# A planned two-layer trunk: decay products in halves, statistics from a copy, a norm with another last tile, and PSUM reads ordered in the plan

## The chip, the cores and the metric

The kernel runs on one core of a Trainium2 chip. The metric is device microseconds of one execution, lower is better. TensorE is called PE below, VectorE DVE, ScalarE ACT, SyncE SP; PSUM is the buffer into which PE writes and from which DVE and ACT read.

## The reference

Two layers of a trunk run on 128 context tokens and 512 latent tokens of width 1024, float32. A layer is a modulated norm, one wide input projection, three mixers side by side (attention A, gated DeltaNet B, chunked gMLP C), a gated merge and an output projection. What the change touches:

```python
def _rms(x, g):                       # the norm ahead of a layer
    y = xf * lax.rsqrt(jnp.mean(xf * xf, axis=-1, keepdims=True) + EPS)

def _gdn_chunk(q, k, v, g, beta, s0): # B, per head: decays from cumulated gates, then a scan over chunks
    gc = jnp.cumsum(blk(g), axis=-1)
    ...
    def step(S, xs): ...
    S, o = lax.scan(step, s0, (qc, kc, u, w, gc, decay))

def _chunk_mlp(u, v, p):              # C: mean and variance over 512 channels of each token
    mu = jnp.mean(vf, axis=-1, keepdims=True)
    var = jnp.mean(jnp.square(vf - mu), axis=-1, keepdims=True)
    vn = ((vf - mu) * lax.rsqrt(var + EPS) * p['cm_ln_g'] + p['cm_ln_b'])
```

## The kernel before

All 640 tokens are the columns of every tile, in two halves of 320 (HF) where a PSUM bank of 512 columns asks for it, or in five groups of 128. The dense products of the projections (tiles `dn`) are three matmuls of 128x320 each (`hh` with `hi`, `hl` with `hi`, `hh` with `lo`), since a float32 factor is split into a rounded part and a rest. They make up most of PE's work, and they are laid between the small products of the mixers, whose inputs come from chains over DVE and ACT.

The program isn't issued as it is written. Every call is recorded (class Recorder). `add` notes for each operation which earlier ones it must follow: those that touch the same part of a tile where one of the two writes. `cost` gives it a duration, and `plan` runs a list of ready operations per engine against these durations, priorities from the place in the program, and the number of buffers of each tile name. `issue` then emits them engine by engine in the planned order, all from line 371, so that a profile tells operations apart by their tiles alone. On the chip an engine works through its order without change, and semaphores hold an instruction until its inputs and its buffer are there. Tiles of PSUM come in three kinds with two buffers each: `dn` (dense), `mm` (small products) and `p` (two banks; `p2()` in the code). A PSUM tile counts as one whole in `add` (box, line 93).

Places that the change touches:

- `gdn_head` (line 908), once per head, four per layer. For its decays PE multiplies triangular masks scaled by the gates (G, four tiles) with a constant (`c_strict`) into one `p` tile, in pieces of 512 and 128 columns; ACT takes the exponential of all 640. Then q and k of the head are transposed into `p` tiles (p_687 and p_688 in the rows below), whose squares ACT sums (`junk`, five each) before the next products of the head, p_698, can take the buffer that p_687 leaves. The scan of the head before runs at the same time: products Q and qkv, Q and G, V and G into `mm` tiles (mm_624 to mm_638), each waiting for DVE or ACT.
- The gMLP statistics (lines 1224 to 1236): for five groups of tokens PE transposes four tiles `ya` into a `dn` tile, DVE takes mean and variance from it (`bn_stats`, then `bn_aggr`), and ACT copies it to a tile D in SBUF.
- `norm_add` (line 711) squares a tile on ACT and adds it on DVE to a sum, for all tiles but the first and the last; the last square stays by itself, and `norm_end` (line 721) adds up both over the channels on PE. At the end of a layer the new tiles come in pairs from `two_blocks`, and the last pair is 6 and 7.
- Attention is untouched in the text. There a tile `p` is read by DVE (`G<-p,l_q_col,c_ropeT`) and by ACT (two squares, `G<-p 64x640` and `32x640`).

Of the kernel before, what the change touches and what calls it, by code (L numbers as in the profile page):

```python
# [10 lines left out]
AF = mybir.ActivationFunctionType  # L11
# [7 lines left out]
HF = 320  # L19
KM = 8  # L20
# [39 lines left out]
class Recorder:  # L60
# [57 lines left out]
    def add(self, eng, meth, args, kw):  # L118
        op = Op()
        op.n, op.eng, op.meth, op.args, op.kw = len(self.ops), eng, meth, args, kw  # L120
        op.prio = op.n - self.off
        op.preds, op.succs, op.tiles = set(), [], []
        outs, ins = [], []
        for i, x in enumerate(args):
            if isinstance(x, bass.AP):
                (outs if i == 0 else ins).append(x)
        for k, x in kw.items():
            if isinstance(x, bass.AP):
                (outs if k == "accum_out" else ins).append(x)
        for w, aps in ((False, ins), (True, outs)):  # L130
            for ap in aps:
                nm = ap.tensor.name
                if nm not in self.tag:
                    continue
                p0, p1, m = self.box(ap)
                lst = self.acc.setdefault(nm, [])
                keep = []
                for a_ in lst:
                    q, qw, q0, q1, qm = a_
                    hit = (w or qw) and q0 < p1 and p0 < q1 and (m & qm)  # L140
                    if hit and q is not op:
                        op.preds.add(q.n)
                    if not (w and p0 <= q0 and q1 <= p1 and (qm & ~m) == 0 and q is not op and q.eng != "SP"):
                        keep.append(a_)
                keep.append((op, w, p0, p1, m))
                self.acc[nm] = keep
                u = self.users.setdefault(nm, [])
                if not u or u[-1] is not op:
                    u.append(op)
                if nm not in op.tiles:  # L150
                    op.tiles.append(nm)
        self.cost(op, outs, ins)
        self.ops.append(op)
# [269 lines left out]
def trunk_kernel(ctx: ExitStack, tc: tile.TileContext, a, o, depth=DEPTH, dump=None):  # L423
    nc = tc.nc
    rec = Recorder(tc)
    V, S, G, PE, SY = (rec.engine(e) for e in ("V", "S", "G", "PE", "SP"))
# [16 lines left out]
    def p1():  # L443
        return T([P, 512], "mm", pool=ps, bufs=2)
# [4 lines left out]
    def X(tag, shape, dt=F32):  # L449
        return T(shape, tag, dt, bufs=NB[tag])  # L450
# [11 lines left out]
    def R(shape):  # L462
        return X("R", shape)
# [20 lines left out]
    strict = T([P, 2, P], "c_strict", F32R, pool=const)  # L484
# [223 lines left out]
    STREAMS = ((0, NL, 0), (NL, NT, 1))  # L708


    def norm_add(k):

        if k == 0:
            nsum[0] = X("C", [P, NT])
        sq = nsum[0] if k == 0 else X("C", [P, NT])
        S.activation(sq, xt[k], AF.Square)
        if 0 < k < KM - 1:
            V.tensor_tensor(nsum[0], nsum[0], sq, ALU.add)
        return sq

# [67 lines left out]
    def layer(l, md, hh, hl, fill, side):  # L788
# [46 lines left out]
        pt = p1()  # L835
# [72 lines left out]
        def gdn_head(h, qT, kT, vT):  # L908
# [3 lines left out]
            pd = p2()  # L912
            for d in range(2):
                c_ = 4 * d + h
                gx = [X("G", [P, 5, P], F32R), X("G", [P, 5, P], F32R)]
                for t in range(5):
                    S.activation(gx[0][:, t, :], masks[:, (LE, GE)[d], :], AF.Copy, scale=gh.bitcast(F32)[:, t, c_ : c_ + 1])
                V.tensor_tensor(gx[1], masks[:, (LE, GE)[d], :].unsqueeze(1).broadcast_to([P, 5, P]), gl[:, :, c_ : c_ + 1].broadcast_to([P, 5, P]), ALU.mult)
                for n in range(2):
                    gf = gx[n].rearrange("p a b -> p (a b)")  # L920
                    for c0, c1 in ((0, 512), (512, 640)):
                        PE.matmul(pd[:, c0:c1], strict[:, d, :], gf[:, c0:c1], start=(d == 0 and n == 0), stop=(d == 1 and n == 1))
            Bc = X("G", [P, 5, P])
            S.activation(Bc.rearrange("p a b -> p (a b)"), pd[:, 0:640], AF.Exp)


            junk = T([P, P], "junk", bufs=1)
# [89 lines left out]
            for step in range(4):  # L1017
                for d in range(2):
                    t = step if d == 0 else 3 - step
# [38 lines left out]
            for t0, t1 in ((0, 4), (4, 5)):  # L1058
                n = (t1 - t0) * P
# [163 lines left out]
        with rec.hp():  # L1223
            vnt = []
            mv = T([P, 5, 2], "mv", bufs=1)
            for t in range(5):
                pt = pdense()
                for q in range(4):
                    PE.transpose(pt[:, q * P : (q + 1) * P], gv[q][:, t * P : (t + 1) * P], ident)
                st6 = T([P, 6], "st6", bufs=2)  # L1230
                V.bn_stats(st6, pt)
                V.bn_aggr(mv[:, t, :], st6)
                vx = X("D", [P, 512])
                S.copy(vx, pt)
                vnt.append(vx)
            lv = R([P, 5])
            V.tensor_scalar(lv, mv[:, :, 1], 4.0 * EPS, None, ALU.add)
            lrs = rsqrt(lv, R([P, 5]), R([P, 5]))
            for t in range(5):
                V.tensor_scalar(vnt[t], vnt[t], mv[:, t, 0:1], lrs[:, t : t + 1], ALU.subtract, ALU.mult)  # L1240
# [21 lines left out]
        for q in range(4):  # L1262
            zc = silu_block(B_ZC + q, "D")
            V.tensor_tensor(cu[q], cu[q], zc, ALU.mult)
            for t0, t1 in ((0, 4), (4, 5)):
                n, cs = t1 - t0, slice(t0 * P, t1 * P)
# [150 lines left out]
        pt = p1()  # L1417
# [219 lines left out]
        for m in range(KM):  # L1637
            xo = X("qkv", [P, NT])
            SY.dma_start(xo, xsrc[m])
            xn = T([P, NT], f"ya{m}", bufs=1)  # L1640
            if m % 2 == 0:
                outs = []
            outs.append((xn, xo))

            def evac(i, acc, c0, c1):
                xn, xo = outs[i]
                cuts = ((0, c1, 0),) if c0 == 0 else ((c0, NL, 0), (NL, c1, 1))
                mi = m - m % 2 + i
                for b0, b1, s in cuts:
                    V.scalar_tensor_tensor(xn[:, b0:b1], acc[:, b0 - c0 : b1 - c0], md.gate[:, mi, s : s + 1], xo[:, b0:b1], ALU.mult, ALU.add)  # L1650

            if m < 2:
                dense(wsplit(wo(m, 0)) + wsplit(wo(m, 1)), yh, yl, lambda acc, c0, c1: evac(m, acc, c0, c1))
                done = [m]
                if m == 1:
                    B = sums()
            elif m % 2 == 0:
                continue
            else:
                two_blocks([wo(m - 1 + i, half) for i in range(2) for half in range(2)], B, evac)  # L1660
                done = [m - 1, m]
            for n in done:
                xn = outs[n % 2][0]
                if last:
                    SY.dma_start(o["y"][:, n, :], xn)
                else:
                    xt[n] = xn
                    xsrc[n] = spill(xn)
                    sq = norm_add(n)
        return None if last else sq  # L1670


# [16 lines left out]
    for k in range(KM):  # L1689
        sq = norm_add(k)  # L1690
# [10 lines left out]
    for l in range(depth):  # L1701
# [3 lines left out]
        sq = layer(l, mods[l], [h[0] for h in hs], [h[1] for h in hs], fill, side)  # L1705
# [104 lines left out]
```

## Time and profile before

| | |
|---|---|
| time, median of 3 runs | 1702.54 us (1701.52 to 1705.32) |
| the profiled execution | 1704.07 us |
| its span, first to last instruction | 1702.3 us |
| mean granted clock of TensorE | 0.987 |
| PE busy | 1646.9 us (97%) |
| DVE busy | 1287.8 us (76%) |
| ACT busy | 884.9 us (52%) |

The profiled execution took 1.8 us more than its span, and 1.5 us more than the median. Busy time is a sum over the whole span. How the engines stand in one stretch is told by the windows, and what an engine waited for by the idle time ahead of an instruction, with the one that released it. A granted clock of 1 is 2.4 GHz, of 0.5 1.2 GHz.

### The profile page before, as it was taken

The numbers are of one execution on the slowest core, as the hardware profiler recorded it, in microseconds if no ns is written. First come the engines' busy times: TensorE is split into PE (matmuls) and PEld (weight loads), VectorE is DVE, ScalarE is ACT, GpSimd is POOL, SyncE is SP. The second block draws the span as 40 slices with busy tenths as digits, with TensorE's granted clock in tenths as the row PEclk, the third lists the DMA queues.
The fourth block names the chain that finished last, engine by engine and source line by source line (L and its number), as shares of the span: only waits on it lengthen the run. The fifth ranks groups of instructions, "written<-read, shape, count | busy, mean of one in ns | idle before, by whom it ended". The sixth has DMA issues, their size and how long they took to land.

```text
span 1702.3 us, 34983 instructions
## 1 busy us (share of the span) xinstructions
PE 1646.9 (97%) x13286; PEld 1538.8 (90%) x13286; DVE 1287.8 (76%) x3638; ACT 884.9 (52%) x2201; POOL 16.6 (1%) x100
## 2 busy tenths in 40 slices
PE   6999999999999999999999999999999999999998
PEld 5998988999888889999989989889988888899998
DVE  4898888565655777887987988885656557779898
ACT  3566665554544554444445676645545445545453
POOL 0000000000000000000000000000000000000000
PEclk9999999999999999999989999999999999999999
DMA  9311211221111213564542212112221122123252
GB/s 295 99 54 51 62 57 44 70 63 59 47 58 49 84 59 107 157 201 153 189 154 59 61 42 62 57 57 64 69 59 40 53 63 74 52 83 101 85 168 80
DMA packets 94617, 146.39 MB, mean 86 GB/s; under 512 B 14064, under 2 KB 38000, under 8 KB 94448
## 3 DMA queue, kind: packets, MB, share of 16 engines
q1 hardware_dynamic: 94448, 144.15, 27.5%
q8 instruction: 105, 1.72, 0.4%
q14 instruction: 64, 0.52, 0.1%
HBM read 132.28 MB, written 11.83 MB: 85 GB/s over the span
## 4 chain that ended last, share of the span: by engine, by line
PE 84%; DVE 8%; ACT 6%; issue 1%; DMA 0%; SPq 0%; DVEq 0%; ACTq 0%
PE dn L371 44%; PE p L371 24%; PE mm L371 16%; ACT iv L371 2%; DVE lo L371 1%; DVE iv L371 1%; DVE C L371 1%; ACT G L371 1%; DVE G L371 1%; ACT hi L371 1%; DVE ya L371 1%; ACT V L371 1%; DVE mx L371 1%; ACT C L371 1%; DVE D L371 0%
## 5 line engine op out<-in xcount | busy, mean ns | idle before, releaser
L371 PE MATMUL dn<-hh,hi 128*128 128x320 f32 (+1 forms) x1472 | 469.5, 319 | 7.7 <-ACT hh L371 4.2
L371 PE MATMUL dn<-hh,lo 128*128 128x320 f32 (+1 forms) x1472 | 470.8, 320 | 0.0
L371 PE MATMUL dn<-hl,hi 128*128 128x320 f32 (+1 forms) x1472 | 468.9, 319 | 0.0
L371 PEld LDWEIGHTS dn<-hh,hi 128*128 128x128 f32 (+1 forms) x1472 | 276.9, 188 | 14.6 <-ACT hh L371 5.6
L371 PEld LDWEIGHTS dn<-hl,hi 128*128 128x128 f32 (+1 forms) x1472 | 277.5, 189 | 5.1 <-issue 2.8
L371 PEld LDWEIGHTS dn<-hh,lo 128*128 128x128 f32 (+1 forms) x1472 | 277.5, 189 | 3.6 <-issue 1.8
L371 ACT CAST hi<-raw 128x512 fp32r<-128x512 f32 (+1 forms) x300 | 185.8, 619 | 179.0 <-PE dn L371 79.1
L371 DVE TENSOR_TENSOR lo<-raw,hi 128x512 fp32r<-128x512 f32 (+1 forms) x300 | 205.7, 686 | 66.6 <-ACT hi L371 61.5
L371 PE MATMUL dn<-qkv,hi 128*128 128x320 f32 x768 | 176.4, 313 | 0.0
L371 PEld LDWEIGHTS dn<-qkv,hi 128*128 128x128 f32 x768 | 129.8, 189 | 2.5 <-ACT hi L371 1.6
L371 PE MATMUL dn<-qkv,lo 128*128 128x320 f32 x384 | 120.1, 313 | 0.0
L371 ACT CAST hi<-D 128x512 fp32r<-128x512 f32 x88 | 54.6, 621 | 108.0 <-PE dn L371 55.4
L371 PE MATMUL p<-hh,hi 128*128 128x320 f32 x296 | 92.2, 312 | 0.6 <-ACT hi L371 0.6
L371 PE MATMUL p<-hl,hi 128*128 128x320 f32 x296 | 92.2, 312 | 0.2 <-DVE hl L371 0.2
L371 PE MATMUL p<-hh,lo 128*128 128x320 f32 x296 | 92.1, 311 | 0.0
L371 DVE TENSOR_REDUCE mx<-p 128x1 f32<-128x640 f32 x64 | 52.6, 821 | 50.1 <-PE p L371 50.1
L371 ACT ACTIVATE V<-p,mx,scl 128x640 f32<-128x640 f32 x64 | 56.6, 884 | 58.2 <-DVE mx L371 53.1
L371 PEld LDWEIGHTS dn<-qkv,lo 128*128 128x128 f32 x384 | 72.7, 189 | 0.0
L371 ACT COPY V<-p 128x640 f32<-128x640 f32 x64 | 44.6, 698 | 49.3 <-PE p L371 49.1
L371 PE MATMUL p<-G,G 128*128 128x512 f32 x128 | 66.1, 598 | 4.1 <-ACT G L371 4.1
L371 PE MATMUL p<-G,hi 128*128 128x320 f32 x286 | 69.4, 308 | 0.0
L371 ACT ACTIVATE th<-dn 128x320 f32<-128x320 f32 x112 | 48.7, 435 | 39.7 <-PE dn L371 39.5
(350 smaller groups left out, 3471.7 us busy)
## 6 DMA issues: line engine op xcount, KB each, us to landing
raw<-in_w_in SPq DMA_DIRECT2D x212, 256.0 KB, 2.7
G<-in_w_mod SPq DMA_DIRECT2D x96, 256.0 KB, 4.2
raw<-in_w_branch SPq DMA_DIRECT2D x48, 256.0 KB, 2.8
D<-in_w_in SPq DMA_DIRECT2D x32, 256.0 KB, 3.4
ld<-sp SPq DMA_DIRECT2D x16, 320.0 KB, 3.1
raw<-in_w_o SPq DMA_DIRECT2D x20, 256.0 KB, 3.0
G<-in_w_uq SPq DMA_DIRECT2D x16, 192.0 KB, 2.8
D<-in_w_o SPq DMA_DIRECT2D x12, 256.0 KB, 3.9
```

The source lines that it names most:

```text
L371: op.ins = getattr(getattr(nc, ENG[op.eng]), op.meth)(*op.args, **op.kw)
```

## The change

There are four edits. In `add`, a PSUM tile's readers on two different engines are now ordered too, in the order of the program. In `gdn_head` the decays are two pieces of 320 columns in two banks. In the gMLP ACT copies first, and DVE takes the statistics from the copy. In the norm at a layer's end tile 7 is added before tile 6, so that tile 6 is the last.

```diff
--- before.py
+++ after.py
@@ -137,7 +137,7 @@
                 keep = []
                 for a_ in lst:
                     q, qw, q0, q1, qm = a_
-                    hit = (w or qw) and q0 < p1 and p0 < q1 and (m & qm)
+                    hit = (w or qw or (self.tag[nm][1] and q.eng != op.eng)) and q0 < p1 and p0 < q1 and (m & qm)
                     if hit and q is not op:
                         op.preds.add(q.n)
                     if not (w and p0 <= q0 and q1 <= p1 and (qm & ~m) == 0 and q is not op and q.eng != "SP"):
@@ -708,13 +708,13 @@
     STREAMS = ((0, NL, 0), (NL, NT, 1))
 
 
-    def norm_add(k):
+    def norm_add(k, end=KM - 1):
 
         if k == 0:
             nsum[0] = X("C", [P, NT])
         sq = nsum[0] if k == 0 else X("C", [P, NT])
         S.activation(sq, xt[k], AF.Square)
-        if 0 < k < KM - 1:
+        if k not in (0, end):
             V.tensor_tensor(nsum[0], nsum[0], sq, ALU.add)
         return sq
 
@@ -918,10 +918,10 @@
                 V.tensor_tensor(gx[1], masks[:, (LE, GE)[d], :].unsqueeze(1).broadcast_to([P, 5, P]), gl[:, :, c_ : c_ + 1].broadcast_to([P, 5, P]), ALU.mult)
                 for n in range(2):
                     gf = gx[n].rearrange("p a b -> p (a b)")
-                    for c0, c1 in ((0, 512), (512, 640)):
-                        PE.matmul(pd[:, c0:c1], strict[:, d, :], gf[:, c0:c1], start=(d == 0 and n == 0), stop=(d == 1 and n == 1))
+                    for hf in range(2):
+                        PE.matmul(pd[:, 512 * hf : 512 * hf + HF], strict[:, d, :], gf[:, HF * hf : HF * hf + HF], start=(d == 0 and n == 0), stop=(d == 1 and n == 1))
             Bc = X("G", [P, 5, P])
-            S.activation(Bc.rearrange("p a b -> p (a b)"), pd[:, 0:640], AF.Exp)
+            S.activation(Bc.rearrange("p a b -> p (a b)").rearrange("p (c b) -> p c b", c=2), pd.rearrange("p (c b) -> p c b", c=2)[:, :, 0:HF], AF.Exp)
 
 
             junk = T([P, P], "junk", bufs=1)
@@ -1228,10 +1228,10 @@
                 for q in range(4):
                     PE.transpose(pt[:, q * P : (q + 1) * P], gv[q][:, t * P : (t + 1) * P], ident)
                 st6 = T([P, 6], "st6", bufs=2)
-                V.bn_stats(st6, pt)
-                V.bn_aggr(mv[:, t, :], st6)
                 vx = X("D", [P, 512])
                 S.copy(vx, pt)
+                V.bn_stats(st6, vx)
+                V.bn_aggr(mv[:, t, :], st6)
                 vnt.append(vx)
             lv = R([P, 5])
             V.tensor_scalar(lv, mv[:, :, 1], 4.0 * EPS, None, ALU.add)
@@ -1658,7 +1658,7 @@
                 continue
             else:
                 two_blocks([wo(m - 1 + i, half) for i in range(2) for half in range(2)], B, evac)
-                done = [m - 1, m]
+                done = [m, m - 1]
             for n in done:
                 xn = outs[n % 2][0]
                 if last:
@@ -1666,7 +1666,7 @@
                 else:
                     xt[n] = xn
                     xsrc[n] = spill(xn)
-                    sq = norm_add(n)
+                    sq = norm_add(n, KM - 2)
         return None if last else sq
```

The first edit changes no instruction, but the planned order of all engines. Three places are shown. Rows are in an engine's order: operation, written tile, read tiles, and a count where the same stands several times in a row.

Place one is the end of the scan of the second head, in the first layer, on PE. Before:

```order
L371 MATMUL dn_744<-hh_127_195,lo_742 128x320
L371 MATMUL p_679_747<-G_748,c_strict_73 128x512
L371 MATMUL p_679_747<-G_748,c_strict_73 128x128
L371 MATMUL p_679_747<-G_749,c_strict_73 128x512
L371 MATMUL p_679_747<-G_749,c_strict_73 128x128
L371 MATMUL mm_637<-Q_636,G_570 128x128
L371 MATMUL p_679_747<-G_750,c_strict_73 128x512
L371 MATMUL p_679_747<-G_750,c_strict_73 128x128
L371 MATMUL p_679_747<-G_751,c_strict_73 128x512
L371 MATMUL p_679_747<-G_751,c_strict_73 128x128
L371 MATMUL mm_638<-V_579,G_319 128x128
L371 MATMUL p_687_755<-c_ident_68,qkv_711 128x128 x2
```

and now:

```order
L371 MATMUL mm_623<-V_579,G_319 128x128
L371 MATMUL mm_623<-V_580,G_320 128x128
L371 MATMUL dn_744<-hh_127_195,lo_742 128x320
L371 MATMUL p_679_747<-G_748,c_strict_73 128x320 x2
L371 MATMUL mm_624<-Q_616,qkv_255 128x128
L371 MATMUL mm_624<-Q_616,qkv_243 128x128
L371 MATMUL p_679_747<-G_749,c_strict_73 128x320 x2
L371 MATMUL p_687_755<-c_ident_68,qkv_711 128x128 x5
L371 MATMUL mm_626<-Q_625,G_570 128x128
L371 MATMUL p_679_747<-G_750,c_strict_73 128x320
L371 MATMUL mm_628<-Q_627,G_318 128x128
```

The last dense rows (dn_744) stood behind mm_635, and p_687 behind mm_638; now the last of them stands ahead of mm_624, and p_687 two scan steps earlier, ahead of mm_626. On ACT, where `Q_640` is a square of another head's output and `V_579` and `V_580` belong to the scan, it read before:

```order
L371 ACTIVATE V_580<-mm_637,br_249_317 128x128
L371 ACTIVATE G_752<-p_679_747 128x640
L371 ACTIVATE junk_753,ssq_754<-p_687_755 128x128
L371 ACTIVATE Q_640,ssz_639<-V_581 128x128
L371 ACTIVATE junk_753,ssq_754<-p_687_755 128x128
L371 ACTIVATE Q_640,ssz_639<-V_581 128x128
L371 ACTIVATE junk_753,ssq_754<-p_687_755 128x128
L371 ACTIVATE Q_640,ssz_639<-V_581 128x128
L371 ACTIVATE junk_753,ssq_754<-p_687_755 128x128
L371 ACTIVATE Q_640,ssz_639<-V_581 128x128
L371 ACTIVATE C_746<-C_745 128x644
L371 ACTIVATE Q_640,ssz_639<-V_581 128x128
```

and now:

```order
L371 ACTIVATE junk_753,ssq_754<-p_687_755 128x128 x3
L371 ACTIVATE G_752<-p_679_747 128x640
L371 ACTIVATE junk_753,ssq_754<-p_687_755 128x128
L371 ACTIVATE V_579<-mm_633,br_249_317 128x128
L371 ACTIVATE junk_753,ssq_754<-p_687_755 128x128
L371 COPY G_763<-p_688_756 128x640
L371 ACTIVATE C_746<-C_745 128x644
L371 ACTIVATE junk_753,ssq_754<-p_688_756 128x128 x2
L371 ACTIVATE V_580<-mm_637,br_249_317 128x128
L371 ACTIVATE junk_753,ssq_754<-p_688_756 128x128 x3
L371 ACTIVATE Q_640,ssz_639<-V_581 128x128 x4
```

The five squares of p_687 stood alternately with those of Q; now the squares of p_687 are ahead, with V_579 between the fourth and the fifth, and those of Q stand behind p_688's.

Place two is a latent tile of attention on PE: p_1138 takes the transposed probabilities, p_1140 is the next product and takes the buffer that DVE and ACT read. Before:

```order
L371 MATMUL dn_1604<-qkv_1555,hi_1601 128x320
L371 MATMUL p_1138_1206<-c_ident_68,V_1203 128x128 x5
L371 MATMUL dn_1604<-qkv_1556,hi_1601 128x320
L371 MATMUL dn_1604<-qkv_1555,lo_1602 128x320
L371 MATMUL dn_1611<-hh_69_137,hi_1606 128x320
L371 MATMUL dn_1611<-hl_70_138,hi_1606 128x320
L371 MATMUL dn_1611<-hh_69_137,lo_1607 128x320
L371 MATMUL p_1140_1208<-G_1179,G_1153 128x512
L371 MATMUL p_1140_1208<-iv_1175,G_1153 128x128
```

and now:

```order
L371 MATMUL p_1138_1206<-c_ident_68,V_1203 128x128 x5
L371 MATMUL dn_1611<-hh_93_161,hi_1606 128x320
L371 MATMUL dn_1611<-hl_94_162,hi_1606 128x320
L371 MATMUL dn_1611<-hh_93_161,lo_1607 128x320
L371 MATMUL dn_1611<-hh_107_175,hi_1609 128x320
L371 MATMUL dn_1611<-hl_108_176,hi_1609 128x320
L371 MATMUL dn_1611<-hh_107_175,lo_1610 128x320
L371 MATMUL dn_1611<-hh_110_178,hi_1609 128x320
L371 MATMUL dn_1611<-hl_111_179,hi_1609 128x320
L371 MATMUL dn_1611<-hh_110_178,lo_1610 128x320
L371 MATMUL dn_1611<-hh_124_192,hi_1609 128x320
L371 MATMUL dn_1611<-hl_125_193,hi_1609 128x320
L371 MATMUL p_1140_1208<-G_1179,G_1153 128x512
```

Between the transposes and the next product there were five dense rows, and now there are eleven; the next latent tile changes in the same way (five, now eleven), and a third one keeps its count (six ahead of the transposes and nine behind them, now fifteen ahead).

Place three is the gMLP on DVE, where `iv` tiles belong to the inverse of a head and `lo` is the rest of a split weight. Before:

```order
L371 BN_STATS st_582_650<-dn_649 128x6
L371 STREAM_SHUFFLE iv_540<-iv_541 128x80
L371 BN_AGGR mv_648<-st_582_650 128x2
L371 TENSOR_TENSOR lo_673<-raw_671,hi_672 128x512
L371 STREAM_SHUFFLE iv_543<-iv_540 128x10x15
L371 BN_STATS st_585_653<-dn_652 128x6
L371 TENSOR_TENSOR iv_543<-iv_543,iv_542 128x10x15
L371 BN_AGGR mv_648<-st_585_653 128x2
```

and now:

```order
L371 BN_STATS st_582_650<-D_651 128x6
L371 TENSOR_TENSOR lo_673<-raw_671,hi_672 128x512
L371 BN_AGGR mv_648<-st_582_650 128x2
L371 TENSOR_TENSOR iv_543<-iv_543,iv_542 128x10x15
L371 BN_STATS st_585_653<-D_654 128x6
L371 TENSOR_TENSOR iv_542<-iv_542,iv_543 128x10x15
L371 BN_AGGR mv_648<-st_585_653 128x2
```

The statistics read the copy D instead of dn, and the products of `iv` stand closer around them.

## Rows read from the trace of the kernel before

**Rows 1.** Page, busy time of the engines, and the chain that ended last by engine and line

```profile
PE 1646.9 (97%) x13286; PEld 1538.8 (90%) x13286; DVE 1287.8 (76%) x3638; ACT 884.9 (52%) x2201; POOL 16.6 (1%) x100
...
PE 84%; DVE 8%; ACT 6%; issue 1%; DMA 0%; SPq 0%; DVEq 0%; ACTq 0%
```

**Rows 2.** Waits of PE: who was waited for, us in total, times, longest us

```profile
PE p L371 <- DVE C L371: 14.0, 2, 13.3
PE p L371 <- ACT junk L371: 7.1, 2, 3.5
PE p L371 <- ACT iv L371: 5.5, 4, 2.3
...
PE dn L371 <- ACT hh L371: 4.2, 3, 2.3
PE p L371 <- ACT G L371: 4.1, 6, 0.7
```

**Rows 3.** Timeline of PE, one decay: start us, us, engine, line, operation, count

```profile
87.31 0.31 PE L371 MATMUL dn<-hh,hi 128*128 128x320 f32 x1
...
87.75 1.49 PE L371 MATMUL p<-G,c_strict 128*128 128x512 f32 x8
89.08 0.39 PE L371 MATMUL p<-c_ident,qkv 128*128 128x128 f32 x2
```

**Rows 4.** Timeline, gMLP statistics of the first layer (in brackets: idle before, releaser)

```profile
156.59 0.70 DVE L371 BATCH_NORM_STATS2 st<-dn 128x6 f32<-128x512 f32 x1
...
157.32 0.59 ACT L371 COPY D<-dn 128x512 f32<-128x512 f32 x1 [0.94 <-DVE st L371]
...
157.96 0.65 PE L371 MATMUL dn<-c_ident,ya 128*128 128x128 f32 x4 [0.62 <-ACT D L371]
...
159.33 0.70 DVE L371 BATCH_NORM_STATS2 st<-dn 128x6 f32<-128x512 f32 x1 [0.95 <-ACT D L371]
```

**Rows 5.** Timeline, end of the second head's scan, first layer

```profile
235.12 0.61 PE L371 MATMUL mm<-Q,qkv 128*128 128x128 f32 x4
...
242.49 0.40 PE L371 MATMUL dn<-hh,lo 128*128 128x320 f32 x1
...
244.75 0.39 PE L371 MATMUL mm<-V,G 128*128 128x128 f32 x2
...
245.50 0.28 ACT L371 ACTIVATE junk<-p 128x128 f32<-128x128 f32 x1 [0.32 <-PE p L371]
...
249.15 0.26 ACT L371 ACTIVATE junk<-p 128x128 f32<-128x128 f32 x1
...
249.55 2.50 PE L371 MATMUL p<-qkv,qkv 128*128 128x128 f32 x10 [3.54 <-ACT junk L371]
...
256.47 0.39 PE L371 MATMUL dn<-hh,hi 128*128 128x320 f32 x1
```

**Rows 6.** Windows over the same: busy us of each engine (instructions), then granted clock

```profile
235.12:244.75 9.63, 9.63 (x74) 9.46 (x73) 8.54 (x21) 6.99 (x20) 0.22 (x1) 1.00 0.09 28
242.49:256.47 13.98, 10.44 (x58) 8.99 (x57) 10.45 (x45) 9.65 (x43) 2.07 (x4) 0.76 0.28 86
```

**Rows 7.** Timeline, a latent tile of attention, first layer

```profile
420.55 0.88 DVE L371 SCALAR_TENSOR_TENSOR G<-p,l_q_col,c_ropeT 128x640 f32<-128x640 f32 x1
...
421.46 1.41 ACT L371 ACTIVATE G<-p 64x640 f32<-64x640 f32 x2 [1.61 <-DVE G L371]
...
422.92 0.70 PE L371 MATMUL p<-G,G 128*128 128x512 f32 x1 [0.67 <-ACT G L371]
```

**Rows 8.** Timeline, boundary between the layers

```profile
869.79 0.83 DVE L371 TENSOR_TENSOR C<-C,C 128x640 f32<-128x640 f32 x1 [0.80 <-ACT C L371]
...
870.67 2.39 PE L371 MATMUL p<-c_ones,C 128*128 128x1 f32 x20 [0.67 <-DVE C L371]
...
881.41 0.50 PE L371 MATMUL dn<-hh,hi 128*48 128x320 f32 x1 [2.32 <-ACT hh L371]
```

## The prediction, made before the changed kernel ran

> **What bounds the kernel now.** I read the shares and the chain first. TensorE (PE) is busy 1646.9 of 1702.3 us and holds 84% of the chain that ended last; the vector engine (DVE) is busy 1287.8 us [rows 1]. So a change pays only if it takes work off PE, shortens its idle time (1702.3 − 1646.9 = 55.4 us), or keeps its clock up. Second, the waits of PE [rows 2]. 13.3 of the 14.0 us behind DVE's C is the start of the program, which no edit reaches. Of the rest, most comes in pairs, one per layer: "2 times" for `junk`, 7.1 us in all, and 3.5 at the longest. The waits for ACT's G (4.1 us, 6 times) are three per layer. No row names a DMA, so that the transfers which SP now issues in another order are hidden as long as weights come no later than before. Third, the timelines around those waits, one layer each; what I find is counted twice.
>
> **The change, part by part.** The sum is made against the profiled execution, 1704.07 us: the span of 1702.3 and 1.8 us around it, 1.5 us above the median of 1702.54.
>
> *Halves of 320.* Three dense matmuls of 320 columns start within 87.75 − 87.31 = 0.44 us, 0.147 each; the eight matmuls of a head's decay start within 89.08 − 87.75 = 1.33 us [rows 3]. Eight of 320 columns at the dense pace take 8 × 0.147 = 1.18. That is 0.15 less for each of 4 heads in 2 layers, 8 × 0.15 = **−1.2 us**. Columns are the same (2560), so the floor of the edit is zero. The exp still reads 640 elements. By the Trainium skill ("TensorE: Matmul & The Clock Gate", "Wait — 56ns, not 53.3ns?") a matmul's start-to-start time is its columns over 2.4 GHz plus a small constant; by that alone 512 + 128 costs what 320 + 320 does, and the sum would end 1.2 us higher. By that page eight matmuls over 2560 columns would take an estimated 1.09 us; the trace has 1.33, so I hold to the rows.
>
> *gMLP statistics.* The first tile's statistics take 0.70 us from PSUM, ACT's copy then 0.59 after an idle 0.94 behind DVE, and PE's next four transposes stand 0.62 idle for that copy [rows 4]. The two reads of a tile never overlap: in a later one the copy comes first, and the statistics wait 0.95 for it [rows 4]. In the change the buffer is free when the copy is, so PE's 0.62 goes: **−1.2 us** in two layers. Statistics from SBUF are not in this trace; I keep 0.70, and any price from nothing to 0.70 is beside PE's work. The edit adds a wait: DVE's statistics now stand behind ACT's copy, and behind them a `lo` split and the `iv` products of the inverse, which PE waits for. If all five pay the 0.59 that is 3.0 us of DVE time per layer, with other rows in between to fill it; I take none, and range this term from −1.6 to +1.5.
>
> *The plan, end of a head's scan.* This is the largest term and the least certain. Before, PE's last dense row of the stretch is at 242.49, the scan's last product at 244.75, and then PE stands 3.54 us for ACT's `junk`; the dense rows resume at 256.47 [rows 5]. The five `junk` squares run from 245.50 to past 249.15 because those of Q are interleaved [rows 5]. p_698 needs the buffer they read. In the order of the change they stand three and one and one, ahead of Q's, and p_687 itself stands two scan steps earlier on PE. So the 3.54 goes. In exchange 32 dense matmuls that lay beside the scan from 235.12 to 242.49 now stand ahead of it: 32 × 0.147 = 4.7 us, so the scan starts at about 235.12 + 4.7 = 239.8. It took 244.75 − 235.12 = 9.6 us with cover [rows 5]; at that pace it ends at 249.4. Left are ten transposes and a ones product, about 2 us, so the work that ended at 256.47 would end at 251.4. But the clock: 0.76 granted over 13.98 us [rows 6] means 6.7 us at 1.2 GHz instead of 2.4 GHz, after PE stood idle. The new bare stretch, from 239.8 to 251.4, is long and thin too; half pace on those 2 us, and as much again on what follows, costs 2 to 4. That makes 253.4 to 255.4, and a gain of 1.0 to 3.0. I take **−2.0 a layer, −4.0 in all**. DVE limits it on the upper side: it is busy 8.54 of 9.63 and 10.45 of 13.98 [rows 6], so the second stretch can't shrink by more than 3.5. Ends: −3.5 a layer, and below +3.5 if the scan bares all of the 4.7 us and the squares still cost a wait.
>
> *The plan, attention.* PE's p_1140 takes the buffer which DVE's G leaves after 0.88 us and ACT's two squares after 1.41 more, one behind the other: from 420.55 to 422.87 [rows 7]. PE has five dense rows between the transposes and p_1140, and runs dry for 0.67. In the change there are eleven: six more are 0.88 us, over 0.67. The plan before reckoned the two reads as parallel; now it reckons them in a row. A second place changes in the same way; at the third (six and nine dense rows before, fifteen now) the count is equal, and I leave it. Two of three per layer, of 4.1 us over six: 4.1 × 4/6 = 2.7, **−2.6 us**; ends 0 and −4.1.
>
> *The norm's last tile.* Between the layers PE waits 0.67 us for DVE's add of C, which takes 0.83, before the ones product at 870.67; the next dense row follows at 881.41 [rows 8]. Without an add behind the last square that 0.67 goes, but DVE's chain to 881.41 also holds the modulation's copies and adds, some of which now stand in it. I take **−0.5**, ends −0.7 and +0.8.
>
> Sum: −1.2 − 1.2 − 4.0 − 2.6 − 0.5 = −9.5 us. 1704.1 − 9.5 = 1694.6 for a profiled run, and 1702.5 − 9.5 = **1693.0** for the median.
>
> **The rivals.** About 0.2%, 3.4 us, is what a measurement here can tell from no change.
> *A, absorbed.* Freeing PE early helps only if its next inputs come early too. DVE is busy 89% of the scan stretch (8.54 of 9.63) [rows 6]; if it paces this whole part of a layer, the wait behind `junk` comes back elsewhere as one for DVE, and the gMLP and decay terms, in the same part, go with it. What remains is attention and the norm: −3.1, 1699.4, "same". Against it: over the next 13.98 us DVE has 3.5 to spare.
> *B, slower.* The bare scan decides. Its steps of PE, DVE and ACT in turn have no dense row beside them. If the scan at its 9.6 us and the half clock behind it cost 4.5 a layer more than before, instead of 2.0 less, the sum is −5.5 + 9.0 = +3.5: from there it is slower. With the whole 4.7 us bare, and the 6.7 us of half clock once more (3.4 lost), the term is 4.7 + 3.4 − 3.54 = +4.6 a layer: −5.5 + 9.1 = +3.6, 1706.1. For it: the clock row. Against it: small matmuls of p_679, p_687 and p_688 fill the scan.
> *C, more.* The bare stretch ends so early that the clock isn't lowered at all: 6.7 / 2 = 3.4 per layer on top of the 2.0, bounded by DVE at 3.5 in the stretch, so −3.0 more in all and the third attention wait (−1.4) with it: 1688.6.
> *D, the new order is no better.* Both reads of a PSUM tile already stand in a row on the chip [rows 4, 7], so edit one orders nothing new there. If so, the other edits give −2.9: 1699.6, "same".
>
> **Chances.** Forecast 0.52 (1690 to 1698 by its own terms), C 0.12, A 0.13, D 0.09, B 0.14. Faster by over 0.2%: 0.52 + 0.12 = 0.64; same: A and D, 0.13 + 0.09 = 0.22; slower 0.14. Below C are all the best ends, −1.2 − 1.6 − 7.0 − 4.1 − 0.7 = −14.6, which is 1687.9, and two us more for waits that I did not price, such as the 5.5 behind ACT's iv [rows 2]; above, the range takes in A and D and the near half of B: 1686 to 1704.
>
> **What would show it.** Right: eight p<-G,c_strict of 320 columns within 1.18 us; no `junk` row of some 7 us and no ACT D row for the transposes among PE's waits; ACT G's wait down from 4.1 to some 1.4; no DVE C wait at the boundary. Wrong: new PE waits of over 1 us for Q, V or iv in the scan, half clock longer than 6.7 us around it, or DVE waiting for ACT's D ahead of each of the statistics with PE idle behind iv.

## The result, and the profile after

The changed kernel takes 1681.41 us (median of 4 runs, 1679.12 to 1683.82), the kernel before 1702.87 in the same comparison; the ratio of the two is 0.9873 with a 95% interval of 0.9854 to 0.9891. That is 21.5 us, more than twice the 9.5 that were forecast. The profiled execution took 1683.82 us, its span 1681.9.

First the page of the changed kernel, busy time of the engines, and then who PE waited for (us in total, times, longest us):

```profile
PE 1636.5 (97%) x13286; PEld 1538.7 (91%) x13286; DVE 1284.8 (76%) x3638; ACT 890.2 (53%) x2201; POOL 16.7 (1%) x100
```

```profile
PE p L371 <- DVE C L371: 12.9, 1, 12.9
PE p L371 <- DVE iv L371: 6.1, 4, 2.7
PE p L371 <- ACT iv L371: 5.9, 4, 2.6
PE p L371 <- DVE R L371: 2.2, 1, 2.2
PE dn L371 <- ACT hh L371: 2.1, 2, 1.8
...
PE p L371 <- ACT junk L371: 1.1, 2, 0.6
```

PE is busy 1636.5 us instead of 1646.9 [rows 1], and idle 45.4 instead of 55.4. Of the waits of before [rows 2], `junk` fell from 7.1 to 1.1, the waits for `hh` from 4.2 to 2.1, and the six for ACT's G are one of 0.4 (below the rows shown). Longer than before are the waits ahead of tiles p for DVE's iv (6.1, before 0.4) and R (2.2, before 0.4). Those for ACT's iv are about as long (5.9, and 5.5).

Where the time went is read from stages, cut at the same rows in each kernel: the first dense product of a layer, its first p<-D,G (attention begins), the ones product at the boundary, and the end. I call what lies ahead of attention the heads. Windows by these cuts, of before and of after (length, busy us of PE, PEld, DVE, ACT, POOL with counts, granted clock, DMA):

```profile
26.19:363.00 336.81, 325.02 (x3116) 303.96 (x3116) 270.06 (x927) 197.27 (x588) 7.68 (x39) 0.98 0.25 72
363.00:870.67 507.67, 502.66 (x3664) 463.10 (x3662) 372.77 (x895) 242.24 (x511) 0.17 (x3) 1.00 0.35 110
881.41:1209.70 328.29, 316.88 (x2937) 300.68 (x2937) 264.33 (x898) 195.61 (x583) 7.69 (x39) 0.98 0.18 54
1209.70:1702.29 492.59, 483.73 (x3417) 455.86 (x3415) 363.03 (x862) 236.22 (x500) 0.00 (x0) 1.00 0.25 78
```

```profile
26.13:358.32 332.19, 321.27 (x3116) 303.23 (x3116) 269.74 (x927) 198.49 (x590) 7.75 (x39) 0.98 0.26 73
358.32:859.62 501.30, 500.72 (x3658) 463.54 (x3656) 371.60 (x893) 243.92 (x511) 0.34 (x6) 1.00 0.35 110
869.99:1193.81 323.82, 313.24 (x2939) 300.23 (x2937) 264.96 (x906) 196.63 (x585) 7.75 (x39) 0.98 0.19 55
1193.81:1681.95 488.14, 482.13 (x3417) 456.18 (x3415) 361.78 (x861) 237.44 (x500) 0.00 (x0) 1.00 0.26 79
```

The heads are 336.81 − 332.19 = 4.6 us shorter in the first layer and 328.29 − 323.82 = 4.5 in the second; the first layer's attention (with what follows it up to the boundary) is 507.67 − 501.30 = 6.4 shorter, the second's, with the end of the program, 492.59 − 488.14 = 4.5. The boundary gave 0.4. In the first attention window PE's idle time went from 507.67 − 502.66 = 5.0 us to 501.30 − 500.72 = 0.6. The rest of the 6.4 is 1.9 us of "busy" time with the same products (a few records of them are missing in either trace, so that the counts differ).

That rest is a matter of how such a page is read. This is PE in the kernel before, just ahead of the wait of [rows 7]:

```profile
421.95 0.30 PE L371 MATMUL dn<-hh,lo 128*128 128x320 f32 x1
```

The next dense product would have started 0.15 us after 421.95; what stands there is p<-G,G at 422.92, so PE lost 0.97 − 0.15 = 0.82 us, of which the row shows 0.67 as idle, since a product counts as busy for 0.30 us while the next may start after half of it. By this estimate each short wait behind a dense row costs some 0.15 us more than its idle time.

Attention in the changed kernel, the place that answers to [rows 7]:

```profile
416.23 0.88 DVE L371 SCALAR_TENSOR_TENSOR G<-p,l_q_col,c_ropeT 128x640 f32<-128x640 f32 x1
...
417.14 1.41 ACT L371 ACTIVATE G<-p 64x640 f32<-64x640 f32 x2 [1.62 <-DVE G L371]
...
418.51 0.31 PE L371 MATMUL dn<-hl,hi 128*128 128x320 f32 x1
418.66 1.08 PE L371 MATMUL p<-G,G 128*128 128x512 f32 x2
```

ACT's squares still wait 1.62 us for DVE's G, and both still hold the buffer until 418.55. But p<-G,G starts at 418.66 with no idle time ahead of it, 0.15 us after the last of the eleven dense rows that lie there.

The end of the second head's scan, answering to [rows 5] and [rows 6]:

```profile
236.94 0.40 PE L371 MATMUL dn<-hh,lo 128*128 128x320 f32 x1
237.47 0.63 PE L371 MATMUL mm<-Q,qkv 128*128 128x128 f32 x4
...
244.08 1.28 PE L371 MATMUL p<-qkv,qkv 128*128 128x128 f32 x10
...
246.04 0.49 PE L371 MATMUL mm<-V,G 128*128 128x128 f32 x2 [0.23 <-ACT V L371]
...
249.65 0.41 PE L371 MATMUL dn<-hh,hi 128*128 128x320 f32 x1
...
262.14 0.54 PE L371 MATMUL p<-iv,iv 32*32 32x32 f32 x39 [2.69 <-DVE iv L371]
```

```profile
237.00:249.50 12.50, 11.03 (x78) 9.31 (x77) 12.29 (x36) 10.79 (x44) 1.77 (x3) 1.00 0.31 97
262.14:270.00 7.86, 7.75 (x153) 6.82 (x156) 3.63 (x11) 4.39 (x15) 0.00 (x0) 0.78 0.03 12
```

The last dense row is at 236.94, ahead of the scan's product at 237.47, and p<-qkv,qkv at 244.08 has no wait. The dense rows are back at 249.65. DVE is busy 12.29 of 12.50 us, and the clock stays at 2.4 GHz. Then, 12 us later, PE stands 2.69 us for DVE's iv, and in the 7.86 us behind that wait the granted clock is 0.78, which is 2 × 0.22 × 7.86 = 3.5 us at 1.2 GHz. The gMLP, [rows 4], and the decay, [rows 3]:

```profile
87.85 1.34 PE L371 MATMUL p<-G,c_strict 128*128 128x320 f32 x8
89.03 0.60 PE L371 MATMUL p<-c_ident,qkv 128*128 128x128 f32 x4
...
155.67 0.59 ACT L371 COPY D<-dn 128x512 f32<-128x512 f32 x1
...
156.66 0.60 PE L371 MATMUL dn<-c_ident,ya 128*128 128x128 f32 x4
...
156.97 0.68 DVE L371 BATCH_NORM_STATS2 st<-D 128x6 f32<-128x512 f32 x1
```

The eight decay products of 320 columns take 89.03 − 87.85 = 1.18 us. The transposes no longer wait.

### The profile page after: what moved, and what is told of

The parts are those of the page before. It is cut to its first block, busy times and chain, and to the rows that moved or that the text cites. A ratio compares the mean times of both kernels' runs of the same rounds, so it can differ in the third digit from the quotient of the medians.

```text
span 1681.9 us, 34993 instructions
## 1 busy us (share of the span) xinstructions
PE 1636.5 (97%) x13286; PEld 1538.7 (91%) x13286; DVE 1284.8 (76%) x3638; ACT 890.2 (53%) x2201; POOL 16.7 (1%) x100
## 5 line engine op out<-in xcount | busy, mean ns | idle before, releaser
L371 PEld LDWEIGHTS p<-iv,G 32*32 32x32 f32 (+2 forms) x608 | 34.9, 132 | 36.2 <-issue 33.1
```

The source lines that it names most:

```text
L371: op.ins = getattr(getattr(nc, ENG[op.eng]), op.meth)(*op.args, **op.kw)
```

## The experiments

Each kernel ran beside the kernel before on one chip. "Margin" is an entry of SLACKS, nanoseconds that the plan adds before a product's inputs from other engines count as ready. The program plans with 0, 60, 120 and 180 and keeps the plan that it reckons shortest. Before, that is 0; in the changed kernel, and with its first edit alone, it is 60. So the change has a second, hidden part, and the first four runs are there to part the two.

The theories: **R**, ordering the two readers in the plan is the gain, because the second of two readers of a PSUM tile is held until the first is done anyway (1.61 us in [rows 7]), and PE's order now allows for it. **M**, the margin is. **S**, the three other edits are. **L**, a reshuffle by itself is.

The results together, stages from windows as above (heads and attention of the first layer, then of the second):

| run | what it has | median us | ratio [95%] | heads | att. | heads | att. + end |
|---|---|---|---|---|---|---|---|
| kernel before | | 1702.9 | | 336.8 | 507.7 | 328.3 | 492.6 |
| changed kernel | edits 1 to 4, margin 60 | 1681.41 | 0.9873 [0.9854, 0.9891] | 332.2 | 501.3 | 323.8 | 488.1 |
| plan_only | edit 1, margin 60 | 1680.1 | 0.9874 [0.986, 0.9888] | 332.7 | 500.1 | 321.6 | 486.2 |
| plan_slack0 | edit 1, margin 0 | 1678.71 | 0.9863 [0.9848, 0.9878] | 330.9 | 501.6 | 322.0 | 484.4 |
| all_slack0 | edits 1 to 4, margin 0 | 1682.35 | 0.9879 [0.9864, 0.9894] | 335.0 | 501.0 | 324.3 | 487.4 |
| before_slack60 | margin 60 | 1697.41 | 0.9984 [0.9971, 0.9996] | 335.9 | 506.7 | 327.9 | 492.7 |
| before_slack120 | margin 120 | 1697.3 | 0.997 [0.9958, 0.9982] | 336.1 | 504.0 | 327.6 | 488.9 |
| plan_p2 | edit 1 for p | 1695.42 | 0.9959 [0.9946, 0.9972] | 334.7 | 502.1 | 329.0 | 488.7 |
| plan_mm | edit 1 for mm | 1696.08 | 0.9962 [0.9951, 0.9974] | 336.5 | 504.8 | 329.0 | 489.8 |
| plan_dn | edit 1 for dn | 1702.2 | 1.0004 [0.9995, 1.0012] | 334.2 | 510.0 | 325.8 | 495.4 |
| plan_mm_dn | edit 1 for mm and dn | 1695.87 | 0.9954 [0.9942, 0.9966] | 332.4 | 508.1 | 324.2 | 492.3 |
| before_one_reader | one reader for 16 tiles p | 1693.11 | 0.9952 [0.9937, 0.9967] | 334.2 | 502.6 | 328.2 | 488.3 |
| edits_234 | edits 2, 3, 4 | 1694.93 | 0.9951 [0.9939, 0.9963] | 329.0 | 508.7 | 324.8 | 493.6 |
| halves_only | edit 2 | 1704.28 | 1.0008 [0.9999, 1.0017] | 335.3 | 507.9 | 328.3 | 494.1 |
| gmlp_only | edit 3 | 1695.46 | 0.997 [0.9953, 0.9986] | 330.6 | 512.5 | 318.9 | 495.5 |
| plan_halves | edits 1, 2 | 1681.9 | 0.9874 [0.9861, 0.9887] | 330.0 | 500.7 | 323.8 | 487.2 |
| plan_gmlp | edits 1, 3 | 1680.35 | 0.9866 [0.9847, 0.9884] | 329.2 | 502.0 | 321.1 | 486.3 |
| plan_norm | edits 1, 4 | 1677.51 | 0.9859 [0.9841, 0.9876] | 332.5 | 500.8 | 324.6 | 486.9 |
| plan_gmlp_norm | edits 1, 3, 4 | 1677.81 | 0.9859 [0.9839, 0.9879] | 331.9 | 503.4 | 321.4 | 485.3 |
| plan_norm_one_reader | edits 1, 4, one reader | 1681.66 | 0.9883 [0.9868, 0.9898] | 330.9 | 501.6 | 322.6 | 487.3 |

Where no margin is named, it is 0. The stages come from one execution each, the ratios from all. Differences below are by the ratio: 0.001 is 1.7 us.

**The plan and the margin.**

```diff
 hit = (w or qw or (self.tag[nm][1] and q.eng != op.eng)) and ...   # plan_only, plan_slack0
-SLACKS = (0, 60, 120, 180)
+SLACKS = (0,)       # plan_slack0, all_slack0;  (60,) in before_slack60
```

**plan_only**, expected:

> Only the first edit: readers of a PSUM tile on two engines are ordered in the plan; everything else as before. The plan now also takes its margin of 60 ns (SLACKS) where it took 0 before. Theory R (the ordered reads end PE's waits for a second reader, above all in attention, where the changed kernel is 6 us a layer shorter): 1683 to 1690, with the three waits of PE for ACT's G gone in both layers. Theory M (the margin does it) expects the same here. Theory S (the separate edits have their own gains and the plan little): 1699 or more.

**plan_slack0**, expected:

> The first edit with the margin held at 0, so that the plan differs from before by the ordered reads alone. Theory R: within 4 us of the run with the first edit alone and a margin of 60, so 1683 to 1692. Theory M: at least half of the gain is lost, 1694 to 1703. Theory S: 1699 or more.

**before_slack60**, expected:

> The kernel before with the margin held at 60 ns, none of the four edits. Theory R: 1699 to 1706, the waits of PE for ACT's G in attention still there. Theory M: 1680 to 1694. Theory S: 1699 to 1706.

**all_slack0**, expected:

> All four edits with the margin held at 0. Theory R: 1680 to 1687, close to the changed kernel. Theory M: 1690 to 1700. Theory S: about 1682.

The first edit alone gives the whole gain, 0.9874, and with margin 0 it gives 0.9863. The margin without the edit gives 0.9984, 2.7 us, and the four edits at margin 0 come to 0.9879. M and S fall. plan_only came out 3 us below the range that R had given, plan_slack0 4 us below, and before_slack60 has its median, 1697.41, 1.6 us below R's; by its ratio it would be 1700.2.

**Which tiles.**

```diff
-hit = (w or qw) and q0 < p1 and ...
+hit = (w or qw or (self.tag[nm][1] and self.tag[nm][0] in ("p2",) and q.eng != op.eng)) and q0 < p1 and ...
```

("p2" is the name of the tiles p in the code; then ("mm",), ("dn",), and ("mm", "dn").)

**plan_p2**, expected:

> The kernel before, margin 0, with readers ordered in the plan for the tiles p alone (among them attention's 16 which DVE's G and ACT's squares read). Theory R, each wait goes with its own tiles: PE's waits for ACT's G and DVE's G in front of p<-G,G and p<-D,G go, 8 places at 0.7 to 0.9 us, so 1693 to 1698. Rival L (any reshuffle of the plan gives most of the gain): 1676 to 1688, or no change.

**plan_mm**, expected:

> The same for the tiles mm alone (scan products read by ACT's V and DVE's Q, attention's 128x256 products read by ACT's copies and DVE's G). Theory R: PE's six waits for DVE's iv in front of mm<-c_ident,iv go, the scans get closer to the plan, 1688 to 1697. Rival L: 1676 to 1688, or no change.

**plan_dn**, expected:

> The same for the dense tiles dn alone (tanh and its product, statistics and copy, the projections' squares and products). Theory R: the gMLP's 0.62 wait goes in both layers and a few short ones, 1694 to 1701. Rival L: 1676 to 1688, or no change. Over the three kinds theory R expects gains that add up to 18 to 28 us, and rival L doesn't.

**plan_mm_dn**, expected:

> Readers ordered in the plan for the tiles mm and dn, not for p, margin 0. All three kinds gave 24 us, p alone 7, mm alone 6.5, dn alone none: 10 are missing. Theory J (the scans of the heads need mm and dn together; attention needs p): 1686 to 1691, with the stretch from a layer's start to its attention some 5 us shorter in each layer, and attention within 3 us of before. Rival C (the missing part is the clock, which stays up only when the waits of all stretches go): 1694 to 1698, the sum of the two alone.

The stages tell what the totals hide. With the tiles p ordered the first layer's attention is 500 to 503.4 us long, in all nine kernels that have it and two readers; without, and with two readers, it is 504 to 512.5, in nine. For the second layer's attention and the end the two sets are 484.4 to 488.7 and 488.9 to 495.5. With mm and dn ordered, and not p, the heads are 4.4 and 4.1 us shorter, and attention is as before:

```profile
25.76:360.49 334.73, 322.92 (x3115) 301.68 (x3116) 270.07 (x927) 197.53 (x588) 7.68 (x39) 0.99 0.25 73
360.49:862.61 502.12, 500.84 (x3663) 462.91 (x3662) 373.55 (x894) 242.99 (x511) 0.17 (x3) 1.00 0.35 111
```

```profile
25.52:357.92 332.40, 321.91 (x3116) 301.95 (x3117) 269.77 (x927) 197.71 (x592) 7.71 (x39) 0.99 0.25 73
357.92:866.03 508.11, 503.62 (x3664) 464.88 (x3662) 372.42 (x895) 241.81 (x508) 0.17 (x3) 0.99 0.35 109
```

Only 16 of the tiles p matter: a plan that orders just those which DVE's product (G<-p,l_q_col,c_ropeT) and ACT's squares read has the same order on every engine, row by row, as plan_p2 (it was planned, not timed). So for p and attention R holds. For mm and dn it isn't shown. plan_dn gave nothing (1.0004) where R had 1694 to 1701; plan_mm kept the six waits for DVE's iv that R had said would go:

```profile
PE mm L371 <- DVE iv L371: 1.7, 6, 0.3
```

The three kinds add up to 7.0 + 6.5 − 0.7 = 12.8 us where R had 18 to 28. The total of theory J was missed too: 1695.87 instead of 1686 to 1691, inside rival C's range. The two parts give 7.0 and 7.8 us, and together the edit gives 23.3. By the profiled executions the stages add up to more (10.9 and 8.6 us of span), and in plan_slack0 some of the rest is the clock: mean granted clocks of 0.989 and 0.989 against 0.993 in plan_slack0 and 0.987 before. At a clock of 1 − x the span holds 2x at 1.2 GHz: 44 us before, 37 with either part, 23 with the whole edit. That is 7 us less than the two parts' savings would leave, worth at most half of it, 3.5. But that is one execution of each. Over all executions the mean clock is 0.9900 in plan_only and 0.9885 in plan_halves, against 0.9895 and 0.9889 in the kernel before beside them, and both gain 21.5 us. There the clock is not what is missing between the parts' 7.0 + 7.8 = 14.8 us and the whole, so C's reason does not hold either; what is missing stays open.

**The three other edits.**

```diff
+PE.matmul(pd[:, 512 * hf : 512 * hf + HF], ...)                     # edit 2: halves_only
+S.copy(vx, pt); V.bn_stats(st6, vx); V.bn_aggr(mv[:, t, :], st6)    # edit 3: gmlp_only
+done = [m, m - 1]; ... sq = norm_add(n, KM - 2)                     # edit 4;  all three: edits_234
```

**edits_234**, expected:

> The three other edits without the ordered reads: halves of 320, statistics from the copy, tile 6 last. By the prediction's own terms (1.2, 1.2 and 0.5) 1699 to 1700. By theory R, with the changed kernel no faster than the run of the first edit alone, 1699 to 1704. If the separate edits carry the change: 1690 or less.

**gmlp_only**, expected:

> The statistics from the copy alone. The three edits without the plan gave 8 us, in the stretch from a layer's start to its attention. Theory G (this edit is that gain, since the dense buffer goes back earlier and the waits behind the squares of the next head go with it): 1693 to 1697. Theory H (the halves are): 1699 to 1704. The prediction's own term was 1.2.

**halves_only**, expected:

> The halves of 320 alone. Theory H: 1693 to 1697; theory G: 1700 to 1704, with eight matmuls of a head in 1.18 us instead of 1.33 either way (by the Trainium skill's start-to-start rule they would take the same time as before). The prediction's own term was 1.2.

The halves take 1.18 us instead of 1.33 per head, and the kernel is no faster: 1.0008, with 0.9999 as the lower end. (One of its eleven executions took 8974 us, for a reason that nothing here shows; it hardly moves the median and is not in the ratio.) The three edits without the plan give 8.3 us, not the 2.9 of the prediction's terms. Theory H falls. G holds by its median, 1695.46; by the ratio the statistics from the copy are 5 of the 8.3 us, with heads that are 6.2 and 9.4 us shorter, and attention 4.8 and 2.9 longer, in a plan where the readers are not ordered. Most of the first layer's 6.2 doesn't lie at the statistics. The products up to 202.97 us of the kernel before are done 2.5 us earlier in gmlp_only (by 200.50), those up to 253.83 us 6.1 earlier (by 247.77), and between them lay the wait for `junk` of [rows 5]. In gmlp_only, with nothing ordered, no wait for `junk` is left (first row, no idle time ahead of it); in plan_only, with all ordered, both waits are still there (second row):

```profile
244.97 1.28 PE L371 MATMUL p<-qkv,qkv 128*128 128x128 f32 x10
```

```profile
PE p L371 <- ACT junk L371: 6.7, 2, 3.3
```

So that wait comes and goes with the plan, and it isn't shown that the heads owe their gain to the order of two readers.

**plan_halves**, expected:

> Ordered reads and the halves, without the statistics from the copy and the other last tile, margin 0. If the edits' gains add: 1677, 1.2 below the run of the ordered reads at margin 0. If a reshuffle of the plan costs or gives a few us by itself, as the changed kernel being no faster than its first edit alone suggests: anywhere from 1674 to 1684.

**plan_gmlp**, expected:

> Ordered reads and the statistics from the copy, margin 0. Alone the first gave 24 us and the second 5 to 8. If the two are after the same waits in the stretch from a layer's start to its attention (theory O): 1677 to 1683, the stretch no more than 7 us shorter than before in either layer. If they add: 1670 to 1675.

**plan_norm**, expected:

> Ordered reads and tile 6 as the norm's last, margin 0; the order on PE differs from the run with ordered reads at margin 0 in a few dozen rows at the boundary alone. By the prediction's term 0.5 us less than that run's 1678.7, with no wait for the add of C ahead of the ones product; within 1677 to 1680. If the 0.5 is given back behind it: 1678 to 1680 with the first dense row after the boundary as late as before.

**plan_gmlp_norm**, expected:

> The change without the halves, which alone gave nothing; the plan takes margin 0. If the halves are worth nothing in company either: 1677 to 1682, no better than ordered reads alone by what can be told. If they cost the change something: 1675 or less.

None is told apart from the first edit alone, and nothing adds: plan_gmlp's heads are 7.6 and 7.2 us shorter than before, where the first edit alone (margin 0) has 5.9 and 6.3 and the statistics alone 6.2 and 9.4. Theory O holds by its total, and its bound of 7 us was passed by a little. The lowest ratio is 0.9859, of plan_norm and of plan_gmlp_norm; its interval overlaps that of the change, so I can't say that either is better.

**Two readers, or only another plan?**

```diff
-V.scalar_tensor_tensor(n2(qT), h2(pq), qcol[:, 0:1], n2(ropeT), ALU.mult, ALU.mult)
-S.activation(n2(sq[0][up]), h2(pq)[0:64], AF.Square)
-S.activation(n2(sq[1][r0]), h2(pq)[64:96], AF.Square)
+S.copy(n2(qT), h2(pq))
+S.activation(sq[0][up], qT[0:64], AF.Square)
+S.activation(sq[1][r0], qT[64:96], AF.Square)
+V.scalar_tensor_tensor(n2(qT), n2(qT), qcol[:, 0:1], n2(ropeT), ALU.mult, ALU.mult)
```

**before_one_reader**, expected:

> The kernel before, margin 0, no reads ordered. In attention ACT first copies the q product from its p tile into SBUF, and the squares and DVE's product read the copy, so that each of the 16 tiles p has one reader; this adds 16 copies of some 0.70 us on ACT. Theory R (attention was late because the plan gave the buffer back after the longer of two reads that the chip makes one after the other): the plan is right again about these tiles, attention 500 to 504 us instead of 507.7 in the first layer, and 1690 to 1697 in all. Rival Q (the reads' order as such isn't the cause, only the other plan that came of it): attention at 506 or more, 1699 or more.

**plan_norm_one_reader**, expected:

> The same copy on top of ordered reads and tile 6 as the last, margin 0. Theory R: nothing left to gain in attention, within 4 us of 1677.5, since the waits for two readers are already planned around. If the time for which the two reads hold the buffer is a cost of its own, even where the plan knows it: 1673 or less.

**before_slack120**, expected:

> The kernel before with a margin of 120 ns, a plan reshuffled on all engines without any edit (more rows move on PE than in the changed kernel's comparison with before). Theory R: 1697 to 1706, attention not shorter than before by over 3 us. Rival L (a reshuffle gains by itself): 1690 or less.

With nothing ordered and one reader for the 16 tiles, attention takes 502.6 us, as with the readers ordered, and the kernel 1693.11:

```profile
359.78:862.39 502.61, 499.68 (x3663) 462.02 (x3661) 372.81 (x895) 247.91 (x519) 0.17 (x3) 1.00 0.35 111
```

Q falls. For these 16 tiles, and so for attention, the cause is the second reader, and that the plan gave the buffer back as if both read at once. No such run was made for the tiles mm and dn, which the heads use too. On top of the ordered reads the copy gives nothing (0.9883, and 4.2 us above plan_norm's median, just past R's 4): the second reader costs nothing more that shows once it is planned for. L is not all wrong: plans reshuffled without an edit came out 2.7 and 5 us faster (0.9984, 0.997), and in before_slack120 attention happens to be 3.6 us shorter, just past what R had allowed. A few us of any total here are such luck; 24 aren't.

## Why the prediction was wrong

**The attention term failed.** "Two of three per layer, of 4.1 us over six … −2.6 us; ends 0 and −4.1": it measured 6.4 in the first layer and 4.5 in the second with the program's end, about 11. (4.1 × 4/6 is 2.7; 2.6 went into the sum.) The mechanism was right: plan_p2 and before_one_reader, in which nothing but the reads of these tiles is changed, have some 9.4 of it each. The size was read from one row, the wait for ACT's G. Three things were left out. First, the third place was left as it was because its count of dense rows was equal; its wait went as well. Second, the other short waits of PE in the same window, for DVE's G and for iv, belong to it: plan_p2 has none of them either. These rows are the kernel before's, 363 to 666 us, and then all that the changed kernel has from 358.32 to 859.62:

```profile
PE p L371 <- ACT G L371: 2.1, 3, 0.7
PE mm L371 <- DVE iv L371: 0.7, 3, 0.2
PE p L371 <- DVE G L371: 0.7, 1, 0.7
PE mm L371 <- ACT iv L371: 0.2, 1, 0.2
PE p L371 <- DVE V L371: 0.2, 1, 0.2
```

```profile
PE p L371 <- ACT hi L371: 0.3, 1, 0.3
PE p L371 <- DVE hl L371: 0.2, 1, 0.2
```

The five sum to 3.9 us, of 5.0 idle, for one layer, and all of them went, against the 2.05 that I had claimed as the most for a layer (4.1 over two). Third, each of these nine waits costs an estimated 0.15 more than its idle time, 1.4 of the 1.9 us of "busy" time that went. A bound for this term from the idle time of the whole window, 5.0 a layer and 10 in all, would have come near.

**The heads.** Halves, statistics and scan were to give 1.2 + 1.2 + 4.0 = 6.4, and 9.1 were measured, but not by these terms. The halves' step is right and its time is not: the 1.2 us of PE did not reach the end (halves_only), so the upper of its two ends, none, was the true one. The rule of the Trainium skill that I had weighed ("TensorE: Matmul & The Clock Gate", "Wait — 56ns, not 53.3ns?") would make both forms equally long; the trace has 1.18 against 1.33, so it does not describe the pieces of 512 and 128 here, though the time came out as if it did. The statistics were mis-sized: gmlp_only shortens the heads by 6 to 9 us and not by 0.6 a layer, for the most part by another plan at the end of a scan. In company it adds nothing that can be told.

**The scan.** The 3.54 us wait behind `junk` went, as forecast. The dense rows were expected back at 253.4 to 255.4, for the work that ended at 256.47 [rows 5], which includes three of them. They are back at 249.65, so that this work ends at some 250.2 (three at 0.147 us, and the narrow products between): 6.3 us earlier, of which some 2.3 had been gained ahead of the scan, which starts at 237.47 and not at the 239.8 that I had reckoned. Two figures were off. The scan took 246.04 − 237.47 = 8.6 us to its last product instead of the 9.6 taken over from before, and the clock, for which I had charged 2 to 4 us, stayed at 2.4 GHz until the scan's work was done. A part of it is given back behind it: 2.69 us for DVE's iv, with DVE busy 98% of the scan, and the 3.5 us at 1.2 GHz after that. That was rival A's mechanism, at a smaller price. The products up to 310.31 us before are 3.9 earlier in the changed kernel (by 306.40), and not 6.3. In plan_only the wait for `junk` is still there (6.7 us), and its heads are as short. So this wait isn't what sets the length of the heads. What made them 9.1 us shorter instead of 6.4 is not shown.

**The norm.** The wait for DVE's add of C went, and PE waits 2.2 us for R in its place; 0.4 was measured at the boundary against 0.5 forecast, within what single profiles differ by.

**The rivals.** B did not come: the bare scan kept the clock. A and D gave 2.9 to 3.1 and were far off. C, with 1688.6, was the nearest, and its third attention wait went, but its main reason failed: over the heads the mean clock is 0.98 before and after. The range's lower end, 1686, was built from the same 4.1 us as the attention term, and failed with it. Of the 12 us between 9.5 and 21.5, attention's term is some 8 and the heads' 3.

## What to carry to other kernels

When two engines read one PSUM tile, a plan or a schedule has to add the reads up, not take the longer: here that was 1.3% of a kernel in which PE is 97% busy, about half of it in attention, whose text nobody touched. For that half the cause is shown; for the heads' half it is argued. To bound such a term take the idle time of the whole window in which the buffer is passed on, under whatever name the waits stand, and add the part of each wait that the page counts as busy (0.15 us each here). And where a planner picks among plans, look which one it picked before and after: a test with the choice held fixed costs one run and frees the explanation from it.

## What the runs showed of the hardware that I had not expected

Single executions of one and the same order differ by some 5 us, and much of that is the clock. plan_slack0 and plan_norm have the same order up to the boundary. From the first dense product to the first decay they take:

```profile
25.79:85.97 60.18, 59.92 (x530) 53.76 (x531) 49.63 (x131) 29.17 (x70) 0.68 (x12) 1.00 0.52 148
```

```profile
26.09:87.76 61.67, 61.41 (x530) 54.68 (x531) 49.62 (x131) 29.33 (x70) 0.68 (x12) 0.97 0.50 143
```

530 products, 60.18 us at a clock of 1.00 and 61.67 at 0.97. PE had stood idle for 1.75 us just ahead of it in both. 0.03 of 61.67 us is 2 × 0.03 × 61.67 = 3.7 us at 1.2 GHz, which costs up to half of that, 1.8 us; 1.5 were lost. Over the span the mean clock is 0.993 in one and 0.990 in the other, and their spans are 1676.0 and 1681.3 us, though the medians of all runs, 1678.71 and 1677.51, are 1.2 us apart. One kernel shows it as well: plan_norm's four spans are 1681.3 us at a mean clock of 0.990, and 1674.9, 1675.3 and 1675.6 at 0.994.
